# One-core hybrid backbone: key copies put ahead of the next pair's steps on ScalarE, attention pinned to one pattern from its twelfth unit, modulation rows one at a time

## The chip, the cores and the metric

The kernel runs as one program on one core of a Trainium2 chip. The metric is device time in microseconds. The kernel before took 1196.98 us (median of three runs, 1195.08 to 1200.05). Engines are named as in the profile: PE is TensorE (PEld its weight loads), DVE VectorE, ACT ScalarE, POOL GpSimd, SP the queue that issues the DMAs.

## The reference

Two layers over 512 latent tokens of width 1024, with a prefix of 256 context tokens. Layer 0 is grouped-query attention (12 query heads, 4 key heads, head width 64) beside a 2-D Fourier mixing; layer 1 is a convolution module; each is followed by a squared-ReLU MLP.

```
sh1, sc1, g1, sh2, sc2, g2 = adaln_params(s_x, ada_w[i], ada_b[i])   # silu(c) @ ada_w + ada_b
h_x = modulate(rms_norm(x, norm1_g[i]), sh1, sc1)
# layer 0: q, k, v, f = h @ w_in;  k = rope(rms_norm(k) * k_g);  the context's k has no rope
s = einsum("bqkgd,bskd->bkgqs", q, k) * ATTN_SCALE
o = einsum("bkgqs,bskd->bqkgd", softmax(s), v)
x = x + g1 * (concat([o, fourier_mix(f)]) @ w_out)
x = x + g2 * sq_relu_mlp(modulate(rms_norm(x, norm2_g[i]), sh2, sc2), w1[i], w2[i])
```

## The kernel before, in words

Weights and activations are held as a high part rounded to a narrower float and a low remainder, and each product is three matmuls (high by high, high by low, low by high). A weight block arrives as a raw 1 MB tile (`raw`, two buffers in the pool `wraw`); its high part `w[:, 0]` is a rounding copy, its low part `w[:, 1]` is raw minus high. The same two buffers also take the modulation tiles `gv`: 1 MB of `ada_w`, two rows of 1024 per partition, each multiplied by silu(c) and summed along the row by one DVE instruction (L232), which gives one column of the modulation `mods`.

Instructions that are pinned (`pin`) keep the order in which the code writes them on their engine; the others are placed by a list scheduler. Each engine runs its own queue strictly in order.

**Keys.** Six blocks of 128 tokens (0 and 1 context, 2 to 5 latent) have key and value products in PSUM. They are worked off in pairs: squares on ACT (`key_square`), sums and mean on DVE and a log and exp on ACT (`key_sum`), three small DVE steps and then eight ACT copies that scale each head by its root (`key_root`, L682), rope on DVE and two ACT copies into the staging tile `st` (`key_turn`), its low part on DVE (`key_low`), eight PE transposes into the two `tp` banks and two ACT copies from there into `kA` and `kB` (`place_key`, L643 and L647). Between the `place_key` calls PE does query products (`query_slot`, 12 matmuls). Since all of it is pinned, the order on ACT is that of the list of calls from L776 to L846.

**Attention.** A unit is one head and 128 queries; there are 48, in the order of `PAIRS`. Unit n needs four score matmuls into a score bank (two such banks), a row maximum and a scaled negative of it on DVE (L572, L573), an exp with row sum on ACT (L576), a reciprocal on DVE (L578) and a scaling of the probabilities on POOL (L579). Three units later (m = n - 3) `flip` transposes its six 128x128 blocks on PE into the two `tp` banks (L899) and copies them to `PT` (L903 on ACT, L905 on DVE). After every fourth unit twelve matmuls by the values follow (`weigh`, six steps of two, L916), whose result is copied to `act`. Nothing in this loop is pinned. Into it `SPREAD` puts the splitting of the next two weight blocks (high on POOL, low on DVE) in pieces of 512 columns, and `GV_AT` eight modulation tiles of two rows each. Then `w_out` (`residual_gemm`) begins, and from there PE has matmuls to the end of the kernel.

Of the kernel before, what the change touches and what calls it, by code (L numbers as in the profile page):

```python
# [16 lines left out]
P = 128  # L17
# [33 lines left out]
SPREAD = 8  # L51
SPREAD_STEP = 2
# [7 lines left out]
HIGH_POOL = tuple(range(2, 12))  # L60
# [7 lines left out]
GV_AT = (4, 5, 6, 7, 8, 9, 10, 11)  # L68
# [8 lines left out]
def build(tc, xT, ctxT, vec, gbc, rope, dft, dft64, eye, ada1, adat,  # L77
# [149 lines left out]
    def gemv_tile(r):  # L227
# [4 lines left out]
        nc.vector.scalar_tensor_tensor(r, r, 1.0, sbc, ALU.mult, ALU.mult, accum_out=mod(l, j, t))  # L232
# [53 lines left out]
    with ExitStack() as e1:  # L286
# [275 lines left out]
        def softmax(h, qt):  # L562
            kv = h // (NQ // NKV)
            sc = score_bank()
            qs = qT[:, h, qt * P:(qt + 1) * P]
            for a, b in ((0, 512), (512, NK)):
                nc.tensor.matmul(sc[:, a:b], lhsT=qs, rhs=kA[:, kv, a:b], start=True,  # L567
                                 stop=False)
                nc.tensor.matmul(sc[:, a:b], lhsT=qs, rhs=kB[:, kv, a:b], start=False,  # L569
                                 stop=True)  # L570
            sm = ats.tile([P, 4], F32, name="sm", tag="sm", bufs=4)
            nc.vector.tensor_reduce(sm[:, 0:1], sc[:, :NK], AX.X, ALU.max)  # L572
            nc.vector.scalar_tensor_tensor(sm[:, 1:2], sm[:, 0:1], -1.0,  # L573
                                           rq[:, qt, h:h + 1], ALU.mult, ALU.mult)
            p = ats.tile([P, NK], F32, name="p", tag="p", bufs=3)
            nc.scalar.activation(p, sc[:, :NK], AF.Exp, bias=sm[:, 1:2],  # L576
                                 scale=rq[:, qt, h:h + 1], accum_out=sm[:, 2:3])
            nc.vector.reciprocal(sm[:, 3:4], sm[:, 2:3])  # L578
            nc.gpsimd.tensor_scalar(p, p, sm[:, 3:4], 0.0, ALU.mult, ALU.add)  # L579
            return p  # L580

# [15 lines left out]
        with ExitStack() as ei:  # L597
# [62 lines left out]
            def key_sum(n):  # L660
# [6 lines left out]
                pin(nc.vector.tensor_scalar(v, ss, 1.0 / HD, EPS, ALU.mult, ALU.add))  # L667
                pin(nc.scalar.activation(y, v, AF.Ln))
                pin(nc.scalar.activation(y, y, AF.Exp, scale=-0.5))
                key["vy", n] = v, y  # L670

            def key_root(n):
# [5 lines left out]
                for i in range(2):  # L678
                    kn = wk.tile([P, 512], F32, name="kn", tag="kn", bufs=2)[:, :256]
                    for h in range(NKV):  # L680
                        r = slice(h * HD, (h + 1) * HD)
                        pin(nc.scalar.activation(kn[:, r], kv_ps[n + i][:, r], AF.Copy,  # L682
                                                 scale=rk[:, i * NKV + h:i * NKV + h + 1]))
                    key["n", n + i] = kn

            def key_turn(i):
                tt, kn = kv[i][3], key.pop(("n", i))
# [87 lines left out]

            key_square(0)  # L776
            key_sum(0)
            w_lows(w2_parts, 0)
            key_root(0)
# [3 lines left out]
            key_low(0)  # L783
            w_lows(w2_parts, 2)
            key_low(1)
            values(0)
            kv_products(2, 3)
            key_square(2)
            key_sum(2)
            w_lows(w2_parts, 3)  # L790
            key_root(2)
            kv_products(4, 5)
            key_turn(2)
            key_turn(3)
            key_low(2)
            key_low(3)
            key_square(4)
# [3 lines left out]
            for a_ in w3_parts:  # L801
                ws.high(*a_)
            w_lows(w3_parts, 0, 1)
            place_key(0)
            values(2)
            key_sum(4)
            w_lows(w3_parts, 2)
# [7 lines left out]
            query_slot(0)  # L815
            place_key(1)
            key_root(4)
            w_lows(w3_parts, 3)
            query_slot(1)
            place_key(2)  # L820
            key_turn(4)
# [33 lines left out]
        with ExitStack() as ea:  # L855
# [36 lines left out]
            def flip(h, qt, p):  # L892
# [3 lines left out]
                for g, (a, b) in enumerate(((0, 4), (4, 6))):  # L896
                    tp = tbank().rearrange("p (t n) -> p t n", t=4)
                    for i in range(a, b):
                        nc.tensor.transpose(out=tp[:, i - a], in_=p[:, i * P:(i + 1) * P],  # L899
                                            identity=ident)  # L900
                    d = PT[key][:, a:b, (qt % 2) * P:(qt % 2 + 1) * P]
                    if g == 0 or qt % 2 == 0:
                        nc.scalar.activation(d, tp[:, :b - a], AF.Copy)  # L903
                    else:
                        nc.vector.tensor_copy(d, tp[:, :b - a])  # L905
# [3 lines left out]
            def weigh(pair, half, kt):  # L909
# [3 lines left out]
                for j in range(2):  # L913
                    h = 2 * pair + j
                    kv = h // (NQ // NKV)
                    nc.tensor.matmul(po[key][64 * j:64 * j + 64, :],  # L916
                                     lhsT=vS[:, kt, kv * HD:(kv + 1) * HD],
                                     rhs=PT[h, half][:, kt], start=kt == 0, stop=kt == 5)
                if kt == 5:
                    c = slice(half * H, half * H + H)  # L920
                    nc.scalar.activation(act[:, 0, pair, c], po[key], AF.Copy)
                    nc.vector.tensor_tensor(act[:, 1, pair, c], po[key],
                                            act[:, 0, pair, c].bitcast(F32), ALU.subtract)

            work = []
            fourier(0, 0)
            for n in range(len(units) + AHEAD):
                if AHEAD <= n < len(units):
                    score(n)
                m = n - AHEAD  # L930
# [3 lines left out]
                flip(2 * pair + j, qt, ready.pop(m))  # L934
# [7 lines left out]
                for _ in range(2):  # L942
                    if work:
# [554 lines left out]
```

## Time and profile before

| | us |
|---|---|
| median of the runs | 1196.98 |
| the profiled execution, its own time | 1197.75 |
| its span, first to last instruction | 1195.8 |
| PE busy | 1167.5 |
| DVE busy | 766.3 |
| ACT busy | 493.3 |
| POOL busy | 166.8 |

The stages concerned lie between 55.7 us (second half of the key products) and 264.41 us (first matmul of `w_out`). A matmul's end is modelled, so that a row's duration on PE overlaps with the next row; how long PE is held by a group is read from the start of one row to the start of the next.

### The profile page before, as it was taken

Reading aid. Unit: us, or ns where it says so; the run is one execution under the profiler, and the core shown is the slowest. Engines: PE = TensorE matmul, PEld = TensorE weight load, DVE = VectorE, ACT = ScalarE, POOL = GpSimd, SP = SyncE. Lnnn points to the kernel's source line nnn. Section 1 sums busy time; section 2 is a strip of 40 time slices with the busy share of each in tenths; the row PEclk is TensorE's granted clock in tenths of the full one; section 3 lists DMA queues with packets and bytes.
Section 4 is the critical chain, followed back from the end, with each engine's and each line's share of the span. In section 5 each row is a group of like instructions: output and inputs, shape, how many; then the busy total and the mean of one; then the engine's idle time right before and its main releaser. Section 6 shows DMA issues by size and latency. Waiting matters only on the chain.

```text
span 1195.8 us, 16153 instructions
## 1 busy us (share of the span) xinstructions
PE 1167.5 (98%) x6362; PEld 976.7 (82%) x6362; DVE 766.3 (64%) x1372; ACT 493.3 (41%) x895; POOL 166.8 (14%) x202
## 2 busy tenths in 40 slices
PE   6989999999999999999999999999999999999998
PEld 3678766668998888888889988989988888888887
DVE  5966788757976665675555999989853443443431
ACT  5463676652642332232333715577632331331320
POOL 0212354440000000000003138620000000000000
PEclk9989999999999999999999999999999999999999
DMA  9521223336167555455532234423242233223301
GB/s 374 181 71 36 71 83 133 138 106 247 47 236 248 185 200 211 180 197 189 208 141 71 72 133 166 160 76 130 78 141 94 83 106 106 79 98 106 106 18 53
DMA packets 25339, 160.21 MB, mean 134 GB/s; under 512 B 2608, under 2 KB 5680, under 8 KB 6832
## 3 DMA queue, kind: packets, MB, share of 16 engines
q1 hardware_dynamic: 25264, 159.19, 37.4%
q8 instruction: 50, 0.82, 0.3%
q14 instruction: 25, 0.20, 0.1%
HBM read 157.08 MB, written 2.10 MB: 133 GB/s over the span
## 4 chain that ended last, share of the span: by engine, by line
PE 88%; DVE 5%; ACT 2%; POOL 1%; issue 1%; DMA 1%; SPq 1%; DVEq 0%; ACTq 0%
PE mm L193 24%; PE mm L194 24%; PE mm L192 24%; PE mm L1149 3%; PE po L916 2%; PE tp L899 2%; PE po L325 2%; PE sc L325 2%; PE sc L567 1%; POOL p L579 1%; DMA ar<-in_ada 1%; PE sc L569 1%; ACT p L576 1%; PE tp L643 1%; DVE sm L572 1%
## 5 line engine op out<-in xcount | busy, mean ns | idle before, releaser
L193 PE MATMUL mm<-act,w 128*128 128x512 f32 (+1 forms) x992 | 338.2, 342 | 0.6 <-DVE act L1331 0.5
L194 PE MATMUL mm<-act,w 128*128 128x512 f32 (+1 forms) x992 | 337.4, 341 | 0.0
L192 PE MATMUL mm<-act,w 128*128 128x512 f32 (+1 forms) x992 | 337.3, 342 | 0.0
L165 ACT ACTIVATE w<-raw 128x1024 fp32r<-128x1024 f32 (+1 forms) x160 | 153.6, 987 | 232.7 <-PE mm L194 201.2
L168 DVE TENSOR_TENSOR w<-raw,w 128x1024 fp32r<-128x1024 f32 (+2 forms) x176 | 186.2, 1083 | 34.3 <-ACT w L165 25.7
L192 PE MATMUL mm<-f,w 128*128 128x512 f32 (+1 forms) x560 | 207.8, 371 | 0.0
L193 PE MATMUL mm<-f,w 128*128 128x512 f32 (+1 forms) x560 | 207.7, 371 | 0.0
L194 PE MATMUL mm<-f,w 128*128 128x512 f32 (+1 forms) x560 | 207.7, 371 | 0.0
L193 PEld LDWEIGHTS mm<-act,w 128*128 128x128 f32 x992 | 187.8, 190 | 22.5 <-DVE act L1331 1.4
L192 PEld LDWEIGHTS mm<-act,w 128*128 128x128 f32 x992 | 187.2, 190 | 22.4 <-ACT act L1341 0.7
L194 PEld LDWEIGHTS mm<-act,w 128*128 128x128 f32 x992 | 187.8, 190 | 21.3
L1037 DVE SCALAR_TENSOR_TENSOR x<-mm,mods,x 128x512 f32<-128x512 f32 (+1 forms) x82 | 55.8, 684 | 171.4 <-PE mm L194 171.3
L1091 DVE TENSOR_TENSOR rsq<-relu 128x512 f32<-128x512 f32 (+1 forms) x76 | 45.7, 606 | 126.6 <-ACT relu L1088 126.6
L1088 ACT ACTIVATE relu<-mm 128x512 f32<-128x512 f32 (+1 forms) x76 | 40.3, 530 | 196.8 <-PE mm L194 195.7
L192 PEld LDWEIGHTS mm<-f,w 128*128 128x128 f32 x560 | 105.5, 188 | 18.3
L193 PEld LDWEIGHTS mm<-f,w 128*128 128x128 f32 x560 | 105.5, 188 | 18.2
L194 PEld LDWEIGHTS mm<-f,w 128*128 128x128 f32 x560 | 105.5, 188 | 18.0
L232 DVE SCALAR_TENSOR_TENSOR gv<-gv,sbc 128x1024 f32<-128x1024 f32 x80 | 96.5, 1219 | 4.2 <-DMA gv<-in_adat 4.1
L168 POOL TENSOR_TENSOR w<-raw,w 128x1024 fp32r<-128x1024 f32 x12 | 29.9, 2513 | 396.7 <-ACT w L165 396.7
L1138 DVE SCALAR_TENSOR_TENSOR sb<-u,vecs,sb 128x512 f32<-128x512 f32 x112 | 75.3, 749 | 0.0
L579 POOL TENSOR_SCALAR p<-p,sm 128x768 f32<-128x768 f32 x48 | 57.7, 1205 | 70.6 <-DVE sm L578 42.7
L572 DVE TENSOR_REDUCE sm<-sc 128x1 f32<-128x768 f32 x48 | 45.6, 952 | 13.6 <-PE sc L569 10.2
(232 smaller groups left out, 1297.9 us busy)
## 6 DMA issues: line engine op xcount, KB each, us to landing
raw<-in_w SPq DMA_DIRECT2D x64, 1024.0 KB, 4.8
gv<-in_adat SPq DMA_DIRECT2D x40, 1024.0 KB, 5.0
raw<-in_pw SPq DMA_DIRECT2D x12, 1024.0 KB, 4.9
w<-in_diag SPq DMA_DIRECT2D x8, 1152.0 KB, 5.0
ar<-in_ada SPq DMA_DIRECT2D x8, 1024.0 KB, 10.0
raw<-in_w_in SPq DMA_DIRECT2D x6, 1024.0 KB, 4.8
raw<-in_w_out SPq DMA_DIRECT2D x4, 1024.0 KB, 4.8
xx<-in_xT SPq DMA_DIRECT2D x2, 1024.0 KB, 10.6
```

The source lines that it names most:

```text
L165: hi = nc.scalar.activation(w[:, 0, r], raw[:, r], AF.Copy)
L168: eng.tensor_tensor(w[:, 1, r], raw[:, r], w[:, 0, r].bitcast(F32), ALU.subtract)
L192: nc.tensor.matmul(ps, lhsT=whi, rhs=xhi, start=first, stop=False)
L193: nc.tensor.matmul(ps, lhsT=whi, rhs=xlo, start=False, stop=False)
L194: nc.tensor.matmul(ps, lhsT=wlo, rhs=xhi, start=False, stop=last)
L232: nc.vector.scalar_tensor_tensor(r, r, 1.0, sbc, ALU.mult, ALU.mult, accum_out=mod(l, j, t))
L325: i = nc.tensor.matmul(ps, lhsT=a, rhs=w[:, e, k], start=first, stop=last)
L572: nc.vector.tensor_reduce(sm[:, 0:1], sc[:, :NK], AX.X, ALU.max)
L579: nc.gpsimd.tensor_scalar(p, p, sm[:, 3:4], 0.0, ALU.mult, ALU.add)
L1037: nc.vector.scalar_tensor_tensor(xs, ps, mod(l, j, t), xs, ALU.mult, ALU.add)
L1091: nc.vector.tensor_tensor(s, r, r, ALU.mult)
L1138: tap = nc.vector.scalar_tensor_tensor(vs if j == TAPS - 2 else a, u[:, t, j:j + S], w[j], a, ALU.mult, ALU.add)
```

## The change

**Keys.** The log and exp of a pair become a step of their own (`key_log`); the scaling of the keys moves from eight ACT copies per pair to one DVE multiplication per block (`key_scale`, called in `key_turn`). The list of calls is written anew: the squares of pair 2 stand ahead of the staging copies of pair 0, `place_key(0)` and its copies ahead of `key_turn(2)`, `place_key(1)` ahead of `key_low(2)`. The high parts of weight block 3 move from POOL to ACT (`w3_high`), one at a time between the steps.

**Attention.** From unit n = 12 on every instruction of the loop is pinned, in the order scores, share of the unit before, piece of a weight block, transposes and their copies, exp, modulation row, three `weigh` steps in every second unit. The pieces of the two weight blocks are high and low on POOL, at even m from m = 10. The modulation rows come singly at the m of `ROWS_AT`; a tile is requested when the one before is begun. Weight blocks 10 and 11 take their high part on ACT instead of POOL, and `w_out` sums in another order of k.

```diff
-SPREAD = 8
-SPREAD_STEP = 2
-HIGH_POOL = tuple(range(2, 12))
+HIGH_POOL = tuple(range(2, 10))
-GV_AT = (4, 5, 6, 7, 8, 9, 10, 11)
+STEADY = 12
+ROWS_AT = (20, 22, 26, 28, 30, 32, 33, 34, 36, 38, 40, 41, 42, 44, 45, 46)
...
+        def raw_scores(h, qt, on=False):
...
+            held(on, nc.vector.tensor_reduce(sm[:, 0:1], sc[:, :NK], AX.X, ALU.max))
+            held(on, nc.vector.scalar_tensor_tensor(sm[:, 1:2], sm[:, 0:1], -1.0,
+                                                    rq[:, qt, h:h + 1], ALU.mult, ALU.mult))
+            return sc, sm, rq[:, qt, h:h + 1]
+        def powers(sc, sm, r, on=False):
             p = ats.tile([P, NK], F32, name="p", tag="p", bufs=3)
+            held(on, nc.scalar.activation(p, sc[:, :NK], AF.Exp, bias=sm[:, 1:2], scale=r,
+                                          accum_out=sm[:, 2:3]))
+        def shares(p, sm, on=False):
+            held(on, nc.vector.reciprocal(sm[:, 3:4], sm[:, 2:3]))
+            held(on, nc.gpsimd.tensor_scalar(p, p, sm[:, 3:4], 0.0, ALU.mult, ALU.add))
...
-                for i in range(2):
-                    kn = wk.tile([P, 512], F32, name="kn", tag="kn", bufs=2)[:, :256]
-                    for h in range(NKV):
-                        r = slice(h * HD, (h + 1) * HD)
-                        pin(nc.scalar.activation(kn[:, r], kv_ps[n + i][:, r], AF.Copy,
-                                                 scale=rk[:, i * NKV + h:i * NKV + h + 1]))
+            def key_scale(i):
+                kn = wk.tile([P, 512], F32, name="kn", tag="kn", bufs=2)[:, :256]
+                pin(nc.vector.tensor_tensor(heads(kn, NKV), heads(kv_ps[i][:, 0:256], NKV),
+                                            key.pop(("r", i)).unsqueeze(2)
+                                            .to_broadcast([P, NKV, HD]), ALU.mult))
...
+            kv_products(2, 3)
             key_square(0)
             key_sum(0)
+            key_log(0)
             w_lows(w2_parts, 0)
+            key_square(2)
             key_root(0)
...
+            def w3_high(i):
+                _, _, w, raw, r = w3_parts[i]
+                pin(nc.scalar.activation(w[:, 0, r], raw[:, r], AF.Copy))
+            key_log(2)
+            w_lows(w2_parts, 3)
+            w3_high(0)
             place_key(0)
+            key_root(2)
...
             query_slot(0)
+            w3_high(1)
+            key_turn(2)
+            w3_high(2)
+            key_turn(3)
+            w_lows(w3_parts, 0)
             place_key(1)
+            key_low(2)
...
+            def piece():
+                k, _, w, raw, r = ws.later.pop(0)
+                pin(nc.gpsimd.tensor_copy(w[:, 0, r], raw[:, r]))
+                pin(nc.gpsimd.tensor_tensor(w[:, 1, r], raw[:, r], w[:, 0, r].bitcast(F32),
+                                            ALU.subtract))
+            def load_rows():
+                k = gemv_at[0] + len(rows)
+                if k < len(ROWS_AT):
+                    raw = wraw.tile([P, WB], F32, name=f"gv{k}", tag="raw")
+                    nc.sync.dma_start(raw, adat[k // 2])
+                    rows.extend([raw[:, 0:D], raw[:, D:2 * D]])
+            def row():
+                if len(rows) % 2 == 0:
+                    load_rows()
+                gemv_tile(rows.pop(0), True)
...
             for n in range(len(units) + AHEAD):
+                m = n - AHEAD
+                on = n >= STEADY
                 if AHEAD <= n < len(units):
-                    score(n)
+                    pair, _, j, qt = units[n]
+                    new = raw_scores(2 * pair + j, qt, on)
+                if last is not None:
+                    ready[n - 1] = shares(*last, on)
+                if on and ws.later and m % 2 == 0:
+                    piece()
...
+                flip(2 * pair + j, qt, ready.pop(m), on)
+                if new:
+                    last = powers(*new, on)
...
+                if m == ROWS_AT[0] - 2:
+                    load_rows()
+                if m in ROWS_AT:
+                    row()
+                if not on:
+                    for _ in range(2):
+                        if work:
+                            weigh(*work.pop(0))
+                elif m % 2 == 0:
+                    for _ in range(3):
+                        if work:
+                            weigh(*work.pop(0), True)
...
-    residual_gemm(next_w, from_act, 0, 2, Sumsq(), 1, 0, 3, korder=(6, 7, 0, 1, 2, 3, 4, 5),
+    residual_gemm(next_w, from_act, 0, 2, Sumsq(), 1, 0, 3, korder=(6, 7, 4, 5, 0, 1, 2, 3),
```

ACT in the key stage, before, from the second pair's squares to the first copies into `kA` and `kB` (`hsq` squares, `rss_y` log and exp, `kn` scaled keys, `st` staging):

```order
L658 ACTIVATE hsq<-sc 128x256 x2
L862 ACTIVATE d64hl<-d_1218 128x256
L668 ACTIVATE rss_y<-rss_v 128x8
L669 ACTIVATE rss_y<-rss_y 128x8
L682 ACTIVATE kn<-sc,rk 128x64 x8
L696 ACTIVATE st<-kr 128x4x64
L697 ACTIVATE st<-kr 128x4x64
L696 ACTIVATE st<-kr 128x4x64
L697 ACTIVATE st<-kr 128x4x64
L658 ACTIVATE hsq<-sc 128x256 x2
L647 ACTIVATE kA<-tp 128x4x128
L647 ACTIVATE kB<-tp 128x4x128
```

The same stretch now:

```order
L672 ACTIVATE hsq<-sc 128x256 x2
L714 ACTIVATE st<-kr 128x4x64
L715 ACTIVATE st<-kr 128x4x64
L714 ACTIVATE st<-kr 128x4x64
L715 ACTIVATE st<-kr 128x4x64
L726 ACTIVATE vS<-po 128x256 x2
L686 ACTIVATE rss_y<-rss_v 128x8
L687 ACTIVATE rss_y<-rss_y 128x8
L816 ACTIVATE w_619<-raw_620 128x512
L661 ACTIVATE kA<-tp 128x4x128
L661 ACTIVATE kB<-tp 128x4x128
```

The copies of block 0 into `kA` and `kB` no longer stand behind the scaled keys and staging copies of blocks 2 and 3; the eight `kn` rows have left ACT.

PE in the attention at about unit 24, before (`sc` scores, `tp` transposes, `po` products by the values):

```order
L567 MATMUL sc<-kA,qT 128x256
L569 MATMUL sc<-kB,qT 128x256
L899 MATMUL tp<-ident,p 128x128 x4
L916 MATMUL po<-PT,vS 64x256 x4
L899 MATMUL tp<-ident,p 128x128 x6
L916 MATMUL po<-PT,vS 64x256 x2
L567 MATMUL sc<-kA,qT 128x512
```

And now, two units:

```order
L572 MATMUL sc<-kA,qT 128x512
L574 MATMUL sc<-kB,qT 128x512
L572 MATMUL sc<-kA,qT 128x256
L574 MATMUL sc<-kB,qT 128x256
L928 MATMUL tp<-ident,p 128x128 x6
L946 MATMUL po<-PT,vS 64x256 x6
L572 MATMUL sc<-kA,qT 128x512
L574 MATMUL sc<-kB,qT 128x512
L572 MATMUL sc<-kA,qT 128x256
L574 MATMUL sc<-kB,qT 128x256
L928 MATMUL tp<-ident,p 128x128 x6
```

Scores, six transposes and, in every second unit, six matmuls by the values now alternate evenly, where before they came in pieces of two, four and ten.

DVE in the attention where modulation rows fall, before (`sm` softmax statistics, `gv` a modulation row, `w` a weight's low part):

```order
L572 TENSOR_REDUCE sm<-sc 128x1
L905 COPY PT<-tp 128x2x128
L578 RECIPROCAL sm<-sm 128x1
L573 SCALAR_TENSOR_TENSOR sm<-sm,rq 128x1
L168 TENSOR_TENSOR w_1215<-raw_1216,w_1215 128x512 x2
L578 RECIPROCAL sm<-sm 128x1
L572 TENSOR_REDUCE sm<-sc 128x1
```

And now, around the third row, the first of the second tile:

```order
L577 TENSOR_REDUCE sm<-sc 128x1
L578 SCALAR_TENSOR_TENSOR sm<-sm,rq 128x1
L589 RECIPROCAL sm<-sm 128x1
L231 SCALAR_TENSOR_TENSOR gv_1906,mods<-gv_1906,sbc 128x1024
L577 TENSOR_REDUCE sm<-sc 128x1
L578 SCALAR_TENSOR_TENSOR sm<-sm,rq 128x1
L589 RECIPROCAL sm<-sm 128x1
L935 COPY PT<-tp 128x2x128
```

The weight's low parts are gone from DVE, and a row stands in front of the next unit's maximum, so that nothing can pass it.

## Rows read from the trace of the kernel before

**Rows 1.** The page, first part: busy us (share of span) xinstructions.
```profile
PE 1167.5 (98%) x6362; PEld 976.7 (82%) x6362; DVE 766.3 (64%) x1372; ACT 493.3 (41%) x895; POOL 166.8 (14%) x202
```

**Rows 2.** Stretches: length, then busy (instructions) by engine PE PEld DVE ACT POOL, clock, DMA.
```profile
70.20:74.30 4.10, 0.00 (x0) 0.00 (x0) 3.88 (x10) 3.15 (x12) 0.00 (x0) 0.76 0.31 132
74.30:76.30 2.00, 1.98 (x9) 1.98 (x10) 1.93 (x7) 1.78 (x6) 0.00 (x0) 0.50 0.00 0
...
154.49:163.12 8.63, 8.63 (x55) 5.37 (x55) 8.23 (x21) 6.65 (x15) 1.06 (x2) 1.00 0.01 4
163.12:231.49 68.37, 62.63 (x406) 41.54 (x404) 56.38 (x135) 46.62 (x97) 35.81 (x27) 1.00 0.42 141
231.49:264.41 32.92, 32.30 (x214) 21.57 (x212) 18.46 (x48) 22.00 (x45) 14.53 (x16) 1.00 0.23 79
264.41:1195.80 931.39, 927.54 (x4995) 805.25 (x4994) 574.84 (x911) 335.43 (x541) 82.53 (x112) 1.00 0.38 135
```

**Rows 3.** Waits of PE from 50 to 262: total us, times, longest.
```profile
PE tp L643 <- ACT kA L647: 4.2, 1, 4.2
```

**Rows 4.** Timeline of PE, key stage: start, us, engine, line, form [idle before].
```profile
66.39 1.03 PE L643 MATMUL tp<-ident,st 128*128 128x128 f32 x8
...
74.32 1.97 PE L643 MATMUL tp<-ident,st 128*128 128x128 f32 x8 [4.15 <-ACT kA L647]
75.94 4.49 PE L325 MATMUL po<-w,act 128*128 128x512 f32 x12
80.28 1.03 PE L643 MATMUL tp<-ident,st 128*128 128x128 f32 x8
...
87.54 1.03 PE L643 MATMUL tp<-ident,st 128*128 128x128 f32 x8
```

**Rows 5.** Timeline of ACT, key stage.
```profile
69.10 1.75 ACT L682 ACTIVATE kn<-sc,rk 128x64 f32<-128x64 f32 x8 [1.75 <-DVE rk L677]
...
73.67 0.60 ACT L647 ACTIVATE kA<-tp 128x512 fp32r<-128x512 f32 x1
```

**Rows 6.** Groups by form, 40 to 266: xcount | busy, mean ns | idle before.
```profile
L572 DVE TENSOR_REDUCE sm<-sc 128x1 f32<-128x768 f32 x48 | 45.6, 952 | 13.6 <-PE sc L569 10.2 <-PE tp L899 1.8 <-POOL p L579 1.1
L576 ACT ACTIVATE p<-sc,sm,rq 128x768 f32<-128x768 f32 x48 | 47.5, 992 | 10.1 <-DVE sm L573 9.3 <-PE tp L899 0.4
L903 ACT ACTIVATE PT<-tp 128x512 f32<-128x512 f32 x48 | 28.6, 597 | 19.5 <-PE tp L899 19.4
L232 DVE SCALAR_TENSOR_TENSOR gv<-gv,sbc 128x1024 f32<-128x1024 f32 x18 | 21.9, 1215 | 0.0
L168 DVE TENSOR_TENSOR w<-raw,w 128x512 fp32r<-128x512 f32 x17 | 13.3, 803 | 3.5 <-POOL w L156 3.5
L621 DVE TENSOR_TENSOR t<-sc,tq 128x256 f32<-128x256 f32 x2 | 0.8, 416 | 0.0
```

**Rows 7.** Timeline of PE, attention: two scores' group, transposes, products, and the tail.
```profile
193.64 0.48 PE L567 MATMUL sc<-kA,qT 128*128 128x512 f32 x1
...
194.43 0.60 PE L899 MATMUL tp<-ident,p 128*128 128x128 f32 x4
...
195.97 0.87 PE L899 MATMUL tp<-ident,p 128*128 128x128 f32 x6
196.77 0.65 PE L916 MATMUL po<-PT,vS 128*64 128x256 f32 x4
...
261.14 3.34 PE L916 MATMUL po<-PT,vS 128*64 128x256 f32 x24
```

**Rows 8.** POOL over the span, by form: a 128x512 addition of two tiles.
```profile
L1223 POOL TENSOR_TENSOR vsum<-vsum,v 128x512 f32<-128x512 f32 x3 | 3.8, 1280 | 0.2
```

**Rows 9.** Timeline of attention: a scaling on POOL, a small step on DVE.
```profile
138.71 0.92 POOL L579 TENSOR_SCALAR p<-p,sm 128x768 f32<-128x768 f32 x1 [0.96 <-DVE sm L578]
138.85 0.77 DVE L573 SCALAR_TENSOR_TENSOR sm<-sm,rq 128x1 f32<-128x1 f32 x1
```

**Rows 10.** DMA issues of the page: xcount, KB each, us to landing.
```profile
gv<-in_adat SPq DMA_DIRECT2D x40, 1024.0 KB, 5.0
```

More of the change, by code (lines that the diff above doesn't have):

```diff
@@ L231, in gemv_tile @@
         t = k % KT
[L232 removed]
+        i = nc.vector.scalar_tensor_tensor(r, r, 1.0, sbc, ALU.mult, ALU.mult,
+                                           accum_out=mod(l, j, t))
+        if on:
+            pin(i)
         if t < KT - 1:
@@ L560, in build, with held @@
         ats = e1.enter_context(tc.tile_pool(name="ats", bufs=1, side=right, reuse_waits='tile'))
-        def softmax(h, qt):
+        def held(on, i):
+            return pin(i) if on else i
+        def raw_scores(h, qt, on=False):
             kv = h // (NQ // NKV)
@@ L915, in weigh @@
                     kv = h // (NQ // NKV)
-                    nc.tensor.matmul(po[key][64 * j:64 * j + 64, :],
-                                     lhsT=vS[:, kt, kv * HD:(kv + 1) * HD],
-                                     rhs=PT[h, half][:, kt], start=kt == 0, stop=kt == 5)
+                    held(on, nc.tensor.matmul(po[key][64 * j:64 * j + 64, :],
+                                              lhsT=vS[:, kt, kv * HD:(kv + 1) * HD],
+                                              rhs=PT[h, half][:, kt], start=kt == 0,
+                                              stop=kt == 5))
@@ L933, in build @@
                 pair, half, j, qt = units[m]
-                flip(2 * pair + j, qt, ready.pop(m))
+                flip(2 * pair + j, qt, ready.pop(m), on)
+                if new:
+                    last = powers(*new, on)
+                    if not on:
+                        ready[n] = shares(*last)
+                        last = None
                 if m in FOURIER_AT:
@@ L941, in build @@
                     place_query(2, 2 + PLACE_AT.index(m), False)
-                for _ in range(2):
-                    if work:
-                        weigh(*work.pop(0))
-                if m >= SPREAD and m % SPREAD_STEP == 0:
-                    ws.some(1)
+                if m == ROWS_AT[0] - 2:
+                    load_rows()
+                if m in ROWS_AT:
+                    row()
+                if not on:
+                    for _ in range(2):
[5 more added lines that the diff above has]
+                            weigh(*work.pop(0), True)
                 if m % 4 == 3:
                     work += [(pair, half, kt) for kt in range(6)]
-                    if m // 4 in GV_AT:
-                        gemv(1, wraw)
             for w_ in work:
                 weigh(*w_)
-            ws.some(16)
     wpoolB = es.enter_context(tc.tile_pool(name="wB", bufs=2, side=left, reuse_waits='tile'))
```

81 lines of the change are left out of this document (39 added, 42 removed).

## The prediction

> **What bounds the kernel now.** The page comes first: PE is busy for 1167.5 of 1195.8 us [rows 1], so time can only come from stretches in which PE waits or runs at its lower clock. The stretches show where these lie [rows 2]: from the first matmul of w_out at 264.41 to the end PE is busy for 927.54 of 931.39 us, and nothing in the change shortens that. Ahead of it stand one hole, 70.20 to 74.30 with PE at 0.00, and the attention, in which PE is busy for 62.63 of 68.37 us (163.12 to 231.49, units 12 to 37, by the start of their scores) and then for 32.30 of 32.92. The waits say who ends the hole: the copy into kA, once, for 4.2 us [rows 3]. Third comes the timeline [rows 4, 5].
>
> **The keys.** PE's transposes of blocks 0 and 1 share two banks. Those of block 1 could go at 70.2, but block 0 is still in the banks: its copies (L647) stand on ACT behind the eight scaled copies of blocks 2 and 3 at 69.10, which themselves wait for DVE, and behind four staging copies; they start at 73.67 [rows 5]. The hole costs more than itself: the granted clock is 0.50 behind it [rows 2], the 1.2 GHz level, so that the eight transposes hold PE for 75.94 - 74.32 = 1.62 us. From block 0's transposes (66.39) to block 2's (80.28) two rounds take 13.89 us; the next two, 80.28 to 87.54, take 7.26 [rows 4]. The difference, 6.6, is what the hole costs with its clock.
>
> Now the copies of block 0 stand behind one high part of block 3 only, and the banks are free before PE has done its 12 query products. What is late next: blocks 4 and 5. Their staging must be done for transposes that come at 87.54 - 6.6 = 80.9, while DVE has gained six multiplications out of PSUM, which by the nearest row, another multiplication of that size out of PSUM, take 0.416 each [rows 6]: 2.5 us. ACT loses 1.75 per pair [rows 5] and takes four high parts, which more than pays for them. DVE's extra work lies beside the query products as long as it ends by 80.9; at worst all 2.5 show. I take **-6.5**, with -4.0 and -7.0 as ends.
>
> **Units 10 and 11.** From 154.49 to 163.12 DVE is busy for 8.23 of 8.63 us [rows 2]: late queries, Fourier and softmax together. Two low parts that stand there ahead of unit 10's maximum, at a mean of 0.803 [rows 6], go to POOL: **-1.6** (0 if their place is filled, -3.2 if the two behind them count as well).
>
> **Units 12 to 37.** PE's own need is read from start to start [rows 7]: scores 194.43 - 193.64 = 0.79; six transposes 196.77 - 195.97 = 0.80; the last 24 rows of products, twelve matmuls, 264.41 - 261.14 = 3.27, so 1.64 for six. An even and an odd unit are 2 x 0.79 + 2 x 0.80 + 1.64 = 4.82 us, 13 pairs 62.7, against 68.37. Do the others keep up? DVE per pair: two maxima 1.90, one copy out of PSUM like the 0.416 above, four small steps of some 0.15 (an estimate), on average 1.2 modulation rows of 1.215: 4.4. ACT: two exps at 0.992, two copies at 0.597 and smaller ones of about 0.8 together: 4.0 [rows 6]. POOL: two scalings at 0.92 [rows 9], a subtraction that the nearest row puts at 1.28 [rows 8] and a cast at half of that (an estimate, one input for two): 3.8. All are under 4.82, PE stays the bound: **-5.7**. PE's busy time in the stretch, 62.63, says the same, so I know of no more than this; the other end is 0, where the engines still wait for each other as they do now.
>
> **Units 38 to the end.** PE's need is 10 x 0.79 + 13 x 0.80 + 50 matmuls x 0.2725 = 31.9 against 32.92, a gain of 1.0. Against it stand rows at m = 40, 41, 42 and 44, 45, 46: in such a unit DVE needs about 1.6 + 1.2 = 2.8 us where PE needs 2.4, six times 0.4 less what two score banks hide. I take **0**, with -1.0 and +1.5.
>
> **The wait that is added.** The second modulation tile uses the buffer of the last weight block that is split in pieces. Its last piece is on POOL at m = 24 (iteration n = 27) and ends some 5.2 us after that iteration's scores start (scores 0.79, a maximum 0.95 and 0.7 for small steps and hand-overs, an estimate; then scaling 0.92, cast and subtraction 1.9). Only then can SP issue the load; it lands 5.0 later [rows 10], at 10.2. The row at m = 26 stands two iterations on, behind scores that start at 4.82 and a maximum: at about 7.0. DVE waits for 3.2 us, and since all is pinned, the next units' maxima, small steps and copies out of the transposes wait behind it, and PE for them, through the two score banks and the transposes' bank. About 0.7 is hidden: **+2.5**, from 0 (if the pieces run ahead) to +5. Later tiles have four to eight units, over 9 us, and are in time. SP's queue holds only the next tiles and, at the end, the blocks of w_out, which have 20 us to spare; so the two casts moved to ACT and the new order of k count for nothing.
>
> Sum: -6.5 - 1.6 - 5.7 + 0 + 2.5 = -11.3. The profiled execution took 1197.75, which gives 1186.4; it stands 0.8 above the median of the runs, from which the sum gives 1185.7. I say **1186**.
>
> **A rule weighed.** A small DVE step that began at 138.85 took 0.77 us and ended at 139.62, with POOL's scaling that had begun at 138.71 and took 0.92 [rows 9]. The Trainium skill, "SBUF — State Buffer", section "SBUF: two separate sides", says that a DVE instruction with two SBUF inputs and a GpSimd instruction take one port pair by an exclusive lock, held for the whole instruction. By that rule the pieces, three POOL instructions in a row, stand in the way of the pinned small step of each odd unit. This is rival B.
>
> **Rivals.** A: the row at m = 26 is in time, because POOL runs ahead or DVE is later than I think; -13.8, 1183.5. For it: the two instants are 3 us apart in an estimate of 10.
> B: POOL's pieces block DVE. The small step comes at about 5.2 after the even unit's scores, where the subtraction ends, so it costs nothing at 1.28; if the subtraction is held up itself and takes twice that, each of eight pieces costs 1.1 to 1.3: +9.5, 1195.5. Against it: in the row POOL's scaling kept its 0.92, so that it was DVE that waited and not POOL [rows 9].
> C: the hole comes back at blocks 4 and 5, since DVE's chain is late; without the first term: -4.8, 1192.
> D, slower: the pinned pattern turns into a loop through the two score banks. If each engine waits for the one before, two units take scores 0.79, two rows 2.43, a maximum 0.95, a blocked small step 0.77, a copy 0.60 and an exp 0.99, together 6.5 instead of 4.82: 18 pairs give +30, 1216. It decides from 5.7 per pair on, where it eats the 8.1 us of the first two terms. For it: all this is in strict order. Against it: only 16 rows fall on 36 units.
> E: PE's pause behind the late row drops the clock. After the hole of 4.15 us the granted clock was 0.50; the same again costs 6.6 - 4.15, nearly 2.5: 1188.5. The Trainium skill, "TensorE: Matmul & The Clock Gate", section "HAM oscillation — how this bites in real kernels", has a wait for a DMA do just that. The many shorter pauses of the attention, 5.7 us in 163.12 to 231.49, left the clock at 1.00 [rows 2].
>
> **Chances.** The forecast's five terms 0.64, A 0.15, B 0.06, C 0.06, E 0.05, D 0.04. The best ends of all terms sum to -16.9, 1180; the range that holds eight in ten, 1179 to 1193, takes these in with A and E, goes one lower for products that may cost less in even groups, and takes in part of C. A change of 0.5%, 6 us, is about what runs of this kernel can tell: faster is under 1191, which holds for the forecast, A and E nearly whole, 0.82; the same (B, C and the forecast's upper tail) 0.14; slower 0.04.
>
> **What would show it.** No wait of PE on the copies into kA and a granted clock of 1.00 from 66 to 90 confirm the first term; block 4's transposes at about 81. Units 12 to 24 at 4.8 us a pair confirm the third. One wait of DVE for the modulation tile, of about 3 us near the row at m = 26, confirms the fifth. The forecast is wrong if units run at 5.3 a pair, if waits of DVE on POOL add up to several us, or if PE loses more than 2 us at the keys of blocks 4 and 5.

## The result, and the profile after the change

The changed kernel takes 1181.55 us (median of 4 runs, 1180.31 to 1182.75) against 1197.96 for the kernel before, run beside it (1195.08 to 1200.05): a ratio of 0.9871, 95% interval 0.9851 to 0.9891. The forecast was 1186, with 1179 to 1193 as its range: the time is 4.5 below the forecast and near the lower end of the range. The profiled execution spans 1179.1 us, 16.7 less than the 1195.8 of before.

The page's first part, after (busy us, share of the span, instructions), answers to [rows 1]:

```profile
PE 1157.3 (98%) x6362; PEld 976.4 (83%) x6362; DVE 762.6 (65%) x1370; ACT 493.1 (42%) x883; POOL 168.7 (14%) x198
```

The same stretches as in [rows 2], after; from the third on, from the scores of unit 10, of unit 12, of unit 38 and from the first matmul of w_out. Columns: length, then busy (instructions) of PE, PEld, DVE, ACT, POOL, granted clock, DMA share, GB/s.

```profile
70.20:74.30 4.10, 4.10 (x26) 3.56 (x25) 3.98 (x10) 3.75 (x11) 0.00 (x0) 1.00 0.29 122
74.30:76.30 2.00, 2.00 (x13) 1.71 (x11) 1.83 (x8) 1.64 (x5) 0.00 (x0) 1.00 0.00 0
147.45:152.93 5.48, 5.39 (x33) 3.69 (x33) 5.38 (x15) 4.67 (x11) 0.98 (x2) 1.00 0.02 4
152.93:215.22 62.29, 59.93 (x423) 43.88 (x421) 45.42 (x110) 47.19 (x100) 44.79 (x42) 1.00 0.25 85
215.22:247.55 32.33, 30.59 (x221) 22.18 (x219) 27.23 (x65) 21.31 (x45) 18.38 (x12) 1.00 0.44 151
247.55:1179.10 931.55, 927.61 (x4995) 805.48 (x4994) 575.75 (x915) 339.81 (x549) 79.40 (x108) 1.00 0.38 137
```

Compared with [rows 2]: the hole is gone, and with it the lower clock behind it. Units 10 and 11 take 3.15 us less, units 12 to 37 take 6.08 less, the rest of the attention 0.59 less; from w_out on nothing changed (931.55 and 931.39). The score of unit 10 comes at 147.45 where it came at 154.49, 7.04 earlier, although block 0's transposes start 0.19 later. All of it together: 7.04 + 3.15 + 6.08 + 0.59 - 0.16 = 16.7.

PE's timeline at the keys, after; [rows 4] has the same transposes of before:

```profile
66.58 1.03 PE L657 MATMUL tp<-ident,st 128*128 128x128 f32 x8
...
70.20 1.04 PE L657 MATMUL tp<-ident,st 128*128 128x128 f32 x8
71.00 2.98 PE L327 MATMUL po<-w,act 128*128 128x512 f32 x12
73.82 1.03 PE L657 MATMUL tp<-ident,st 128*128 128x128 f32 x8
...
81.06 1.03 PE L657 MATMUL tp<-ident,st 128*128 128x128 f32 x8
```

Block 1's transposes follow the query products at once, and from 66 to 90 us the granted clock is 1.00. From block 0 to block 4 it is 14.48 us, where it was 21.15.

### The profile page after: what moved, and what is told of

It is laid out like the page before. It is cut to its first block, busy times and chain, and to the rows that moved or that the text cites. A ratio compares the mean times of both kernels' runs of the same rounds, so it can differ in the third digit from the quotient of the medians.

```text
span 1179.1 us, 16124 instructions
## 1 busy us (share of the span) xinstructions
PE 1157.3 (98%) x6362; PEld 976.4 (83%) x6362; DVE 762.6 (65%) x1370; ACT 493.1 (42%) x883; POOL 168.7 (14%) x198
## 4 chain that ended last, share of the span: by engine, by line
PE 88%; DVE 7%; ACT 2%; issue 1%; DMA 1%; SPq 1%; POOL 0%; DVEq 0%; ACTq 0%
PE mm L192 25%; PE mm L193 25%; PE mm L191 25%; PE sc L327 3%; PE mm L1219 3%; DVE sm L577 3%; PE po L327 2%; PE po L946 1%; DMA ar<-in_ada 1%; ACT p L584 1%; PE tp L928 1%; PE tp L657 1%; PE sc L572 1%; DVE sm L578 0%; PE sc L574 0%
## 5 line engine op out<-in xcount | busy, mean ns | idle before, releaser
L164 ACT ACTIVATE w<-raw 128x1024 fp32r<-128x1024 f32 (+1 forms) x168 | 158.0, 970 | 232.7 <-PE mm L193 205.0
L167 DVE TENSOR_TENSOR w<-raw,w 128x1024 fp32r<-128x1024 f32 (+2 forms) x168 | 179.5, 1094 | 36.0 <-ACT w L164 27.4
L584 ACT ACTIVATE p<-sc,sm,rq 128x768 f32<-128x768 f32 x48 | 47.8, 995 | 14.4 <-DVE sm L589 9.7
```

What stands on the lines that cost most here:

```text
L164: hi = nc.scalar.activation(w[:, 0, r], raw[:, r], AF.Copy)
L167: eng.tensor_tensor(w[:, 1, r], raw[:, r], w[:, 0, r].bitcast(F32), ALU.subtract)
L584: held(on, nc.scalar.activation(p, sc[:, :NK], AF.Exp, bias=sm[:, 1:2], scale=r, accum_out=sm[:, 2:3]))
```

## The experiments

Their profiles are compared by two lengths, since block 0's transposes start anywhere from 65.98 to 68.34 us in these executions: from there to unit 10's scores (K), and from these to w_out (A). Medians of one kernel differ between sets of runs (the kernel before: 1195.62, 1196.79 and 1198.18), so a difference of one or two microseconds is read from the lengths. Before: K 88.10, A 109.92. After: K 80.87, A 100.10.

**e12_again**: no edit.

> The changed kernel itself, once more, on the chip of these runs. Theory: block 0's transposes to unit 10's scores 80.9 us and from there to w_out 100.1 as in its first profile, whatever the clock did in the first 60 us; time 1180 to 1182. Rival (the key stage or the attention varies between executions, and part of the 16 us is chance): either stretch off by more than 1 us.

1182.73 us, ratio to before 0.9875 (0.9859 to 0.9892); K 80.90, A 100.09. The theory holds for the lengths, which come again within 0.03 us though block 0 starts at 68.10 here; the time is 0.7 above the 1182 that it named.

**e1_keys**: the key stage alone. **e2_attn**: everything else alone. In words instead of the edit's lines:

```
 e1_keys = before + key_log, key_scale, the new order of the key stage
 e2_attn = after  - the same
```

> The kernel before with the change of the key stage alone; attention, rows and pieces as before. Theory (the parts add): the hole at 70 us goes, from block 0's to block 4's transposes 14.5 us instead of 21.1, the score of unit 10 comes 6.7 to 7.0 earlier, units 10-11 keep 8.6 us and units 12-37 keep 68.4; time 6.7 below the kernel before, about 1190.5. Rival (the time saved is given back in attention, since DVE is the bound there and its late work does not come earlier): the score of unit 10 less than 5 us earlier, time above 1193. Rival (part of the 5 us that the forecast was short belongs to the keys): 1188 or less.

> The changed kernel with the key stage of before; only attention, rows, pieces, the two casts and the order of k are the new ones. Theory (the parts add): the hole of 4.2 us stays, clock 0.50 behind it; units 10-11 in 5.5 instead of 8.6, units 12-37 in 62.3 instead of 68.4, from unit 38 to w_out 32.3; time 9.7 below the kernel before, about 1187.5. Rival (the attention's gain needs the scores to start earlier, against a load or a modulation tile at a fixed time): units 12-37 above 64 us, time above 1190.

e1_keys: 1192.43 us, 0.9971 (0.9962 to 0.9981), K 81.44, A 110.01. e2_attn: 1185.05, 0.9919 (0.9903 to 0.9935), K 84.87, A 100.01. By lengths the parts are separate: e1_keys has the 14.48 us of the new key stage from block 0 to block 4 and the attention of before, e2_attn the new attention. That e1_keys has a K 0.57 above the one after belongs to the attention too: from unit 0's scores to unit 10's it is 35.19 us there, 35.21 before and 34.67 after. In e1_keys the score of unit 10 comes only 4.83 earlier, which is the first rival's sign, but block 0 starts 1.83 later there and units 10 and 11 keep their 8.63, so that nothing was given back in the attention. By time the keys are worth 0.29% or 3.5 us, and not 6.7. The key stage of before explains how that can be: e2_attn has it too, and there block 4 follows block 0 after 18.54 us, not 21.15. PE's hole in e2_attn:

```profile
72.96 1.97 PE L657 MATMUL tp<-ident,st 128*128 128x128 f32 x8 [2.37 <-ACT kA L661]
```

It is 2.37 us where [rows 4] has 4.15. The profiles differ some 15 us earlier, in code that both share. First DVE and POOL in the profile of before, then the same in e2_attn (start, us, line, form):

```profile
49.88 2.37 DVE L438 SCALAR_TENSOR_TENSOR xx<-xx,gain,rstd 128x256 f32<-128x256 f32 x4
54.47 3.61 DVE L438 SCALAR_TENSOR_TENSOR xx<-xx,gain,rstd 128x256 f32<-128x256 f32 x4
50.28 3.19 POOL L156 CAST w<-raw 128x512 fp32r<-128x512 f32 x4 [49.24 <-PE sc L325]
54.38 1.64 POOL L606 TENSOR_TENSOR tk<-tabs,gs 128x256 f32<-128x256 f32 x2 [0.90 <-DMA tabs<-in_rope]
55.98 1.81 POOL L606 TENSOR_TENSOR tq<-tabs,gs 128x256 f32<-128x256 f32 x2
```

```profile
50.33 1.67 DVE L440 SCALAR_TENSOR_TENSOR xx<-xx,gain,rstd 128x256 f32<-128x256 f32 x4
53.51 1.67 DVE L440 SCALAR_TENSOR_TENSOR xx<-xx,gain,rstd 128x256 f32<-128x256 f32 x4
50.73 8.71 POOL L155 CAST w<-raw 128x512 fp32r<-128x512 f32 x4 [49.68 <-PE sc L327]
```

Before, the two engines take turns: a step of DVE takes up to 0.83 us beside a cast of 0.81 and up to 0.97 beside POOL's multiplications for `tk` and `tq`, where it otherwise takes 0.48 (the 3.61 for four stands beside these multiplications, not beside the casts). In e2_attn DVE does its sixteen steps from 50.33 to 56.76 without a break, and POOL's first cast alone takes 6.50 us instead of 0.61. In the second case the keys' chain on DVE is done some 3 us earlier, and the hole is shorter. Of the thirteen profiles with these casts on POOL, three have the first case (before, after, e9_even) and ten the second; after and e12_again are the same kernel, so it differs between executions. The Trainium skill, "SBUF — State Buffer", section "SBUF: two separate sides", has one of DVE and GpSimd lock the other out of a shared port pair for a whole instruction; these rows agree with that, though here a cast stands through sixteen instructions in a row and not one.

**e11_act2**: the kernel before, its four casts on ACT.

```diff
...
-                ws.high(*a_)
...
+                nc.scalar.activation(w[:, 0, r], raw[:, r], AF.Copy)
```

> The kernel before with the four casts that POOL does from about 50 us on placed on ACT. In the profiled execution of before these casts took 0.8 each and DVE's scaling steps beside them 3.61 for four instead of 1.67; in others the casts took 2.2 each and DVE kept its 1.67. Theory (which of the two engines is held up there decides how late the keys' chain is, and so how long PE's hole at block 1 is): without the casts DVE is never held up, block 4's transposes come 18.5 us or less after block 0's instead of 21.1. Rival (the hole depends on ACT's order alone): 21 us, as before; the time within 1 of the kernel before in both.

1195.68 us, 0.9983 (0.9971 to 0.9994). Block 4 follows block 0 after 18.51 us; the hole:

```profile
72.06 1.97 PE L643 MATMUL tp<-ident,st 128*128 128x128 f32 x8 [2.30 <-ACT kA L647]
```

The theory holds for the hole: without these casts DVE's steps take 1.67 for four, and the shorter hole is there. The time is 2 us below the kernel before, where both sides had expected it within 1. One profile could have had the shorter hole by chance, but the runs point the same way: the ten of e11_act2 end at 1197.22, and of the thirteen of the kernel before beside them nine are above that. So the hole of before cost some 4 us or 6.7 (18.51 or 21.15 against 14.48), by execution, and the change takes out either. How often each comes in the kernel before is not shown.

**e6_act**: the new order of the keys, but the scaling as ACT's copies.

```diff
-                pin(nc.vector.tensor_tensor(heads(kn, NKV), ..., ALU.mult))
...
+                for h in range(NKV):
...
+                    pin(nc.scalar.activation(kn[:, r], kv_ps[i][:, r], AF.Copy, scale=rk[:, h:h + 1]))
```

> The changed kernel with the scaled copies of the keys back on ACT (four copies of 64 columns for each block) in place of DVE's one multiplication, in the new order of the key stage. Theory (the order made the gain: block 0's copies no longer stand behind the next pair's steps): block 4's transposes 14.5 us after block 0's, no wait of PE, time within 1 of the changed kernel. Rival (the multiplication had to leave ACT, which has 0.9 us more for each block, for the copies to be early): PE waits for the copies into kA or for the staging, 1 to 4 us.

1189.69 us, 0.9934 (0.9917 to 0.9951), against 1182.23 for e7_small beside it, which is the changed kernel but for two details. K is 89.39, longer than before. The rival holds, with more than its 1 to 4 us: PE waits twice, 5.2 us in all. ACT, then PE, in e6_act:

```profile
72.38 0.91 ACT L702 ACTIVATE kn<-sc,rk 128x64 f32<-128x64 f32 x4
74.57 0.42 ACT L716 ACTIVATE st<-kr 128x256 fp32r<-128x256 f32 x1 [1.28 <-DVE kr L645]
74.90 0.40 ACT L717 ACTIVATE st<-kr 128x256 fp32r<-128x256 f32 x1
75.20 0.58 ACT L661 ACTIVATE kA<-tp 128x512 fp32r<-128x512 f32 x1
```

```profile
75.83 1.14 PE L657 MATMUL tp<-ident,st 128*128 128x128 f32 x8 [2.12 <-ACT kA L661]
...
86.45 1.97 PE L657 MATMUL tp<-ident,st 128*128 128x128 f32 x8 [3.11 <-ACT kA L661]
```

Scaling on ACT, rotation on DVE, staging on ACT: ACT waits 1.28 us for the way through DVE, with block 1's copies behind it. After the change the same copies are at 71.87. Behind the hole of 3.11 us the clock was 0.50 from 86.4 to 89.0; behind the wait of 2.12 it was 1.00 from 76 to 80. The reverse, DVE's multiplication in the old order of calls, was not run, nor were the high parts of block 3 moved by themselves, so what these two are worth alone is not shown.

**e3_late**: the second row at m = 25.

```diff
-ROWS_AT = (20, 22, 26, 28, ...
+ROWS_AT = (20, 25, 26, 28, ...
```

> The changed kernel with its second row at m = 25 instead of 22. The second modulation tile then waits for POOL's last piece, as the fifth term of the forecast had assumed, and no longer for a row on DVE. Theory (term five had the right size and the wrong buffer): request at 194.3, landing at 199, the row at m = 26 waits about 3 us on DVE, PE loses 2 to 3 us, the clock stays 1.00; time 1183.5 to 1184.5. Rival E (the pause drops the clock): 2.5 more, 1186 or above, with a granted clock under 0.8 behind the row. Rival (the two score banks and three power tiles absorb the wait): within 0.7 us of the changed kernel, 1181 to 1182.3.

1184.76 us, 0.9907 (0.9891 to 0.9924), A 102.87. The row on DVE, PE behind it, and PE's clock there (columns as above):

```profile
199.96 1.23 DVE L231 SCALAR_TENSOR_TENSOR gv<-gv,sbc 128x1024 f32<-128x1024 f32 x1 [1.94 <-DMA gv<-in_adat]
```

```profile
202.71 0.44 PE L928 MATMUL tp<-ident,p 128*128 128x128 f32 x2 [2.12 <-DVE PT L935]
```

```profile
200.00:204.00 4.00, 1.88 (x16) 1.17 (x16) 3.93 (x10) 1.63 (x4) 1.03 (x2) 0.99 0.43 172
204.00:206.00 2.00, 2.00 (x8) 1.08 (x5) 1.33 (x3) 1.47 (x4) 1.68 (x1) 0.50 0.24 33
206.00:208.00 2.00, 2.00 (x11) 1.87 (x10) 1.15 (x4) 0.46 (x1) 0.00 (x0) 0.67 0.68 274
```

A wait of 1.94 on DVE became 2.12 on PE, with nothing hidden, and the clock fell to 0.50, the 1.2 GHz level. The pair of units from 30 to 31 took 7.44 us instead of 4.49, and the next 5.45 instead of 4.73. In this execution theory and rival E hold together: the two pairs are 3.67 longer with the clock, and A is 2.77 longer, since the row taken from m = 22 gave back 0.88 before. The median, 1184.76, lies between what the theory (up to 1184.5) and rival E (from 1186) had named; its four runs go from 1183.36 to 1186.45, and only the one at 1185.69 was profiled, so that the drop of the clock is not shown for the others.

**e8_two**: two pieces at m = 8, subtractions on DVE.

```diff
+                if m == 8:
+                    for _ in range(2):
...
+                        nc.gpsimd.tensor_copy(w_[:, 0, r_], raw_[:, r_])
+                        nc.vector.tensor_tensor(w_[:, 1, r_], raw_[:, r_], ..., ALU.subtract)
```

> The changed kernel in which the first two pieces are split at m = 8, ahead of the pinned part, with their subtractions on DVE, as two of the four low parts stood in the kernel before. Theory (units 10-11 are shorter because all four low parts left DVE, which is the bound there, 0.8 us each): from the score of unit 10 to that of unit 12 about 7.1 instead of 5.5 us, time 1.6 above the changed kernel, 1183. Rival (the stretch is shorter because its late queries and Fourier work come earlier, beside less; the low parts find gaps): the stretch stays under 6 us, time within 0.6 of the changed kernel.

1181.48 us, 0.9886 (0.9871 to 0.9900). The first two stretches of the attention:

```profile
147.64:155.34 7.70, 6.22 (x37) 4.05 (x36) 6.46 (x15) 5.66 (x13) 0.91 (x1) 1.00 0.01 3
155.34:215.76 60.42, 59.20 (x417) 43.45 (x417) 44.34 (x111) 46.52 (x98) 41.05 (x38) 1.00 0.25 88
```

Units 10 and 11 are 2.22 longer, where the theory says 1.6; but units 12 to 37, with two pieces fewer, are 1.87 shorter. The time is the one that the rival expected, for another reason; by lengths the run stands between the two, K and A together being 0.91 longer than after. What the early stretch gained by losing its low parts is mostly paid later, where the pieces now stand.

**e4_lowdve**: the pinned subtractions on DVE.

```diff
-                pin(nc.gpsimd.tensor_tensor(w[:, 1, r], raw[:, r], ..., ALU.subtract))
+                pin(nc.vector.tensor_tensor(w[:, 1, r], raw[:, r], ..., ALU.subtract))
```

> The changed kernel with the eight subtractions of the pinned pieces on DVE instead of POOL, everything else pinned as it is. Theory (in the pattern DVE has room): a pair with a piece and no row needs two maxima 1.90, a copy 0.42, small steps 0.6, every second time 0.43, and 0.7 for the subtraction, about 3.9 us on DVE against 4.6 of PE; units 12-37 stay at 62.3 within 0.7, the time within 0.7 of the changed kernel. Rival (moving the subtractions to POOL is where the gain of units 12-37 is from): each costs PE its 0.7 to 1.3 us, units 12-37 at 67 or more, time 5 above the changed kernel.

1186.05 us, 0.9904 (0.9886 to 0.9921), 3.3 above e12_again beside it; units 12 to 37 take 66.36, so both were off, the theory more. DVE has the time, as it said, but not then. DVE, then PE:

```profile
165.36 0.69 DVE L963 TENSOR_TENSOR w<-raw,w 128x512 fp32r<-128x512 f32 x1 [1.59 <-POOL w L962]
```

```profile
167.90 0.44 PE L928 MATMUL tp<-ident,p 128*128 128x128 f32 x2 [0.57 <-DVE PT L935]
```

All eight subtractions wait for POOL's cast, 12.7 us in all, and since DVE's pinned order has them ahead of the next maximum, that waits too; PE waits 5.5 us for DVE, in 8 waits.

**e10_pairs**: both rows of a tile in one unit.

```diff
-ROWS_AT = (20, 22, 26, 28, 30, 32, 33, 34, 36, 38, 40, 41, 42, 44, 45, 46)
+ROWS_AT = (20, 24, 28, 32, 36, 40, 44, 46)
...
                 if m in ROWS_AT:
                     row()
+                    row()
```

> The changed kernel, pinned as it is, with both rows of a modulation tile in one unit, at m = 20, 24, 28, 32, 36, 40, 44, 46, instead of single rows. Theory (two rows in a row hold DVE for 2.43 us, and the next maximum comes late for PE, which has only two score banks): each pair of rows costs PE about 1 us more than two single ones, time 5 to 8 above the changed kernel. Rival (DVE's mean load is the same and the four units between make up for it): within 1.5.

1186.52 us, 0.9904 (0.9884 to 0.9925), A 104.65: 4.55 more, and 3.8 by time against e12_again beside it, so that the theory has the direction and names too much (5 to 8). PE waits 0.44 to 0.50 behind six of the eight pairs of rows and 1.15 behind one; near the end it waits 1.40 for POOL's scaling, and the clock falls behind that (0.53 from 247 to 250).

**e5_nopin**: the same emission, not pinned.

```diff
         def held(on, i):
-            return pin(i) if on else i
+            return i
...
```

> The changed kernel, emitted in the same order with the same single rows and pieces, but nothing of units 12 to 50 pinned, so that the scheduler places them as it did before. Theory (the fixed pattern is what lets PE run through): units 12-37 go back to 66 us or more, time 4 above the changed kernel. Rival (single rows and pieces on POOL make the gain, and the scheduler would find as good an order): units 12-37 under 64 us, time within 1.5 of the changed kernel.

1197.12 us, 1.0005 (0.9991 to 1.0019). From unit 0's scores, then as before:

```profile
114.24:153.78 39.54, 34.56 (x210) 27.30 (x208) 30.75 (x60) 23.59 (x53) 23.97 (x26) 0.96 0.23 80
153.78:166.66 12.88, 9.99 (x47) 5.99 (x47) 10.30 (x16) 5.17 (x12) 7.49 (x6) 0.73 0.23 83
166.66:235.34 68.68, 65.51 (x416) 42.68 (x414) 53.99 (x134) 46.88 (x99) 30.45 (x26) 1.00 0.41 138
235.34:265.45 30.11, 30.11 (x213) 22.26 (x212) 15.41 (x43) 21.37 (x46) 10.98 (x12) 1.00 0.06 13
```

The theory holds and falls short: the whole difference to before is gone, though the key stage itself keeps its 14.48 us from block 0 to block 4. Units 12 to 37 take 68.68, as before; besides, pieces and rows moved ahead (POOL is busy for 23.97 us from unit 0 to unit 10, and this stretch takes 39.54 where it took 34.67 after the change), and in units 10 and 11 PE waits for POOL's scaling, 2.9 us at once. Single rows and pieces on POOL are worth nothing without the fixed order.

**e7_small**: order of k and the two casts as before.

```diff
-HIGH_POOL = tuple(range(2, 10))
+HIGH_POOL = tuple(range(2, 12))
...
-korder=(6, 7, 4, 5, 0, 1, 2, 3)
+korder=(6, 7, 0, 1, 2, 3, 4, 5)
```

> The changed kernel with the order of k in w_out and the engine of the two blocks' casts as before. Theory (both count for nothing, as forecast): from unit 38's scores to w_out 32.3 us and to the end as in the changed kernel, time within 0.7. Rival (the order of k lets w_out start on the part of act that is complete earlier): PE waits 0.6 us or more at the start of w_out.

1182.23 us, 0.9870 (0.9853 to 0.9887); K 80.86, A 100.09. The theory holds up to w_out, and its rival's wait at the start of w_out is not there. From w_out to the end it is 932.2, 0.6 longer than after: PE waits 0.68 for DVE 37 us into it. e3_late and e6_act, with the new order of k, have such a wait of 0.36 and 0.39, so it is not put down to the order.

**e9_even**: 14 rows, away from pieces and odd units.

```diff
-ROWS_AT = (20, 22, 26, 28, 30, 32, 33, 34, 36, 38, 40, 41, 42, 44, 45, 46)
+ROWS_AT = (26, 28, 30, 32, 34, 36, 38, 40, 42, 44, 45, 46, 47, 48)
...
-GV_OUT = 1
+GV_OUT = [2, 1, 1, 1]
...
+                if m == 47:
+                    row()
...
```

> The changed kernel with 14 rows in place of 16 in the attention, none beside a piece: at even m from 26 to 44, then m = 45, 46 and two at 47, where no scores are left; the tile that is missing is taken in w_out, two tiles behind its first block. Theory (a row beside a piece and a row at an odd unit each cost PE 0.7 to 0.9): from unit 10 to w_out 96.5 to 97.5 us instead of 100.1, time 2.5 to 3.5 below the changed kernel, 1178 to 1180. Rival (PE's own need is the bound already, or the rows at the end delay w_out): 99.5 or more, time within 0.7.

1180.12 us, 0.9848 (0.9832 to 0.9865), the best of all. Units 10 to 11, 12 to 37, 38 to w_out:

```profile
149.16:154.64 5.48, 5.39 (x33) 3.69 (x33) 5.37 (x15) 4.67 (x11) 0.98 (x2) 1.00 0.02 4
154.64:215.52 60.88, 59.78 (x423) 43.84 (x421) 41.69 (x107) 47.48 (x101) 42.60 (x43) 1.00 0.20 70
215.52:246.43 30.91, 29.90 (x220) 22.13 (x218) 26.70 (x62) 20.93 (x45) 16.69 (x12) 1.00 0.36 124
```

A is 97.27, 2.83 less than after, as the theory says; the time is 2.1 below e7_small's beside it, a little short of the 2.5 to 3.5, with intervals that overlap. The edit also takes two rows out of the attention and the rows off the odd units, so the 2.83 is the sum of these and of the rows beside pieces. PE waits 1.1 us in 60.88. What a row beside a piece does is seen after the change; POOL, DVE, PE:

```profile
186.04 1.81 POOL L590 TENSOR_SCALAR p<-p,sm 128x768 f32<-128x768 f32 x1 [0.44 <-DVE sm L589]
187.80 0.61 POOL L962 CAST w<-raw 128x512 fp32r<-128x512 f32 x1
188.49 1.28 POOL L963 TENSOR_TENSOR w<-raw,w 128x512 fp32r<-128x512 f32 x1
```

```profile
188.76 1.03 DVE L578 SCALAR_TENSOR_TENSOR sm<-sm,rq 128x1 f32<-128x1 f32 x1
```

```profile
190.23 0.44 PE L928 MATMUL tp<-ident,p 128*128 128x128 f32 x2 [0.73 <-DVE PT L935]
```

The row at 185.87 holds the scaling up to 1.81, the piece comes late, and its subtraction holds a small step of DVE's up to 1.03 instead of 0.16; PE waits 0.73. Without these rows the pairs from units 24 and 26 take 4.72 and 4.49 in e9_even, where both took 5.36; the pair from unit 38, behind the rows at m = 33 and 34, takes 4.49 instead of 5.64. The odd row at m = 41 cost nothing of that kind: the pair from unit 44 took 4.72 with it and 4.83 without.

## Why the prediction was right, and where it failed

The sum was -11.3, the profiles differ by 16.7: right in direction and in its large terms, 5.4 too small. Nearly every term came out at or near its better end, and the best ends together were -16.9.

- The keys, -6.5: K shrank by 7.23, 6.67 of it between block 0 and block 4; no wait of PE, clock 1.00, block 4 at 81.06 for about 81. The size is right against the profile from which it was read, whose hole was the long one; against the shorter one it is 4.0. That this profile had the long hole was chance. The reason given was half of it: six multiplications on DVE were booked as a cost that must be hidden, with the order as the gain. e6_act showed that the new order without them is worth nothing (K 89.39).
- Units 10 and 11, -1.6: 3.15, the end named for four low parts. So the term was sized for two low parts where four count; in e8_two putting two of the subtractions back there costs 2.22.
- Units 12 to 37, -5.7: 6.08. Two errors nearly cancel. PE's need was read as 4.82 a pair; undisturbed pairs took 4.49 to 4.73 (from unit 14 at 158.39 to unit 24 at 181.32, five pairs, 22.93), and PE was busy for 59.93, not 62.7. Six transposes with scores behind them held PE for 0.58, not 0.80, and the products of a pair for 1.45, not 1.64, as the rows behind this list show. Against that PE still waits about 2.4 us, which the sum had at nothing. So the mechanism was right, and the closeness of the size is partly luck. That the pattern itself carries the term was assumed, and e5_nopin shows it.
- Units 38 to the end, 0: 0.59, inside its ends.
- The casts and the order of k, nothing: so in e7_small.
- Rival B: POOL's subtractions kept 1.28, and DVE's small steps were held up in two places (0.79 and 1.03), both behind a row beside a piece. Rivals C and D did not come: PE has no wait at blocks 4 and 5, and no pair from unit 12 to unit 45 takes more than 5.64.

PE in the pair from unit 14, after the change, from start to start:

```profile
159.20 0.82 PE L928 MATMUL tp<-ident,p 128*128 128x128 f32 x6
159.78 0.48 PE L572 MATMUL sc<-kA,qT 128*128 128x512 f32 x1
...
161.44 1.52 PE L946 MATMUL po<-PT,vS 128*64 128x256 f32 x12
162.89 0.50 PE L572 MATMUL sc<-kA,qT 128*128 128x512 f32 x1
```

The fifth term, the late row at +2.5, is the step that failed. It rested on the sentence that the second modulation tile uses the buffer of the last weight block that is split in pieces. It uses that of the first tile, which the program frees earlier (behind the row at m = 22, against the piece at m = 24). SP's order of the changed kernel says so; the loads of the first three tiles, with the signals for which each waits:

```
L970 DMA gv0_1851<-in_adat 128x2048 [waits DMAHW2_49,DMAHW0_49,Pool_49]
L970 DMA gv2_1906<-in_adat 128x2048 [waits DMAHW3_49,DMAHW2_49,DVE_49]
L970 DMA gv4_2073<-in_adat 128x2048 [waits DMAHW1_49,Pool_49]
```

The second waits for DVE's row, the third for POOL's piece. In the trace the three requests stand at 174.32, 187.11 and 194.27, each right behind the end of that instruction. DVE's timeline has the end of the row at m = 22 and the row at m = 26:

```profile
187.00 0.08 DVE L231 DVE_READ_ACCUMULATOR gv<-gv,sbc 128x1 f32 x1
...
195.95 1.21 DVE L231 SCALAR_TENSOR_TENSOR gv<-gv,sbc 128x1024 f32<-128x1024 f32 x1
```

Requested at 187.11 and landed at 191.82, the tile is there 4 us before its row, which waits for nothing. That is rival A's outcome, but not for its reason: the pieces did not run ahead. With the assumed buffer, in e3_late, the row waited for 1.94, PE for 2.12, and the two pairs of units there were 3.67 longer, the drop of the clock included: the mechanism exists, but not in this kernel.

Of the 5.4 us the late row is 2.5, units 10 and 11 are 1.55, and the rest is spread over three terms.

## What to carry to other kernels

Before a wait for a buffer is priced, read in the order of the loading queue which engine's signal the load waits for; the rule by which one thinks buffers go round is no substitute. A step that goes through two engines and comes back (scale, rotate, stage) holds whatever stands behind it on the first engine; here the new order gained nothing until the first part went to the second engine. In a pinned pattern the place of each extra instruction counts more than its engine's load: a row at an even unit cost nothing here, and beside a piece 0.6 to 0.9 us.

## What was unexpected of the hardware

- DVE and POOL hold each other up in either direction, and how differs between executions of the same instructions: they take turns (steps of DVE 0.83 instead of 0.48, casts 0.81 instead of 0.61), or POOL's first cast stands for 6.50 us while DVE does sixteen steps at 0.48. The hole of PE some 15 us later was 4.15 us in a profile of the first kind and 2.37 in one of the second.
- Pauses of PE shorter than the hole of before can also cost the clock, and their length alone does not tell which do: behind 2.12 us (e3_late) and behind 1.40 us in a stretch with other pauses (e10_pairs) it was 0.50 to 0.53 for 2 to 3 us; behind another 2.12 (e6_act), behind 1.71 and 1.39 (e4_lowdve) and behind 0.73 and 1.15 it stayed 1.00.
- Block 0's transposes came between 65.98 and 68.34 us. Between 20 and 30 us, a stretch that no edit touches, the granted clock went from 0.51 (e3_late, block 0 at 68.31) to 1.00 (e11_act2, block 0 at 65.98).
